# A transformer layer with two kinds of attention: adaLN's biases as initial values of its sums, the value weights' split in other places, the next key weights' load in another place

## The chip, the cores and the metric

The kernel runs on one core of a Trainium2 chip. Its time is device microseconds from start to end of one execution. Beside the plain runs there is one execution that the hardware profiler recorded; all rows below are from it.

A core has five engines, each with a queue of its own that it works through in order: TensorE (PE; its weight loads are shown apart as PEld), VectorE (DVE), ScalarE (ACT), GpSimd (POOL) and SyncE (SP), which here only issues transfers. An instruction that needs a result of another engine or of a transfer waits at the head of its queue, and all behind it waits too.

## The reference

One layer on a sequence of 1024 tokens with 1024 channels, in float32:

```
def hybrid_layer(x, c_act, w_ada, b_ada, w_in, rel_bias, g_a, g_b, w_out, w_up, conv_w, conv_b, w_down):
    mod = c_act @ w_ada + b_ada                      # c_act = silu(c)
    shift_mix, scale_mix, gate_mix, shift_ffn, scale_ffn, gate_ffn = jnp.split(mod, N_MOD, axis=-1)

    h = modulate(rms_norm(x), shift_mix, scale_mix)  # h * (1 + scale) + shift
    proj = h @ w_in                                  # (1024, 1024) @ (1024, 3072)
    qa, ka, va, qb, kb, vb = jnp.split(proj, cuts, axis=-1)
    oa = chunked_rel_attention(qa, ka, va, rel_bias) # 8 heads of 64
    ob = stick_breaking_attention(qb, kb, vb)        # 8 heads of 64
    mixed = jnp.concatenate([rms_norm(oa) * g_a, rms_norm(ob) * g_b], axis=-1) @ w_out
    x = x + gate_mix[:, None, :] * mixed

    h = modulate(rms_norm(x), shift_ffn, scale_ffn)
    gate, val = jnp.split(causal_depthwise_conv(h @ w_up, conv_w, conv_b), 2, axis=-1)
    return x + gate_ffn[:, None, :] * ((jax.nn.silu(gate) * val) @ w_down)

def reference(x, c, ...):
    x = hybrid_layer(x, jax.nn.silu(c), ...)         # DEPTH = 1
    return rms_norm(x) * final_g
```

The first line is the adaLN modulation: six vectors of 1024, each a product of the activated condition with a 1024x1024 part of `w_ada`, plus a bias. The change touches how the first two of them, shift and scale of the first sub-layer, get their biases, and how the first weights of `w_in` are made ready.

## The kernel before

Matrix products are made of three: each float32 operand is split into a high part in float32r and a low part, the rest; high x high, high x low and low x high are summed. A split is a copy on ScalarE (`wh`, for weights) and a subtraction on VectorE or GpSimd (`wl`).

The program has three parts. The first (lines 212 to 464, "phase 0") normalises x, transposes it, modulates it and makes q and k of the first pair of heads. The second is the attention with all other projections between its steps, the third the feed-forward part. The change lies in the first, with one function of the second.

Phase 0 goes over eight blocks `kb` of 128 channels. For each block `ada_sum(j, s)` on VectorE makes shift (s = 0) and scale (s = 1): the block's rows of `w_ada` lie as a 128x1024 tile `adaw`, and one multiply-reduce (lines 255 and 256, shown as CUSTOM_DVE, with a second instruction that reads the accumulator) sums them with the condition `cbc`. A small 128x1 instruction adds the bias (line 258), for scale also 1 (line 260). `trans0` on TensorE transposes the block of x into PSUM, half by half (`hf`, 512 tokens). `mod_hi` on ScalarE writes the modulated block twice, as high part `H` (line 302) and as float32 `mod` (line 303); `mod_lo` (line 308) subtracts them for the low part, on GpSimd, for block 7 on VectorE. `first_mm` on TensorE adds the block's products to four accumulators `a` (q and k, two halves): twelve products of 128x512 a block. Two buffers of `mod`, three of `t` and three of `adaw` bound how far the engines run apart.

The value weights of the first pairs come in two halves, loaded by `load_v0` (line 328) and split by `split_v0` (line 331), the first half's `wl` on VectorE, the second's on GpSimd, four pieces each. Loaded weights `raw` have two buffers, so that a load waits until the one before the last is split.

Then `evac_q0` and `evac_k0` copy the accumulators out. Each q half also goes by two transfers a head from one tile to another (lines 186 and 187), eight in all, each of which SyncE holds until its copy is there. The second part starts with `prefetch(0)` and `fill`: eight value tiles `mm` of 24 products each (`job_v`, line 498), with two PSUM buffers, whose results go out by two copies on ScalarE (line 512) and two subtractions on VectorE (line 513). `fill` also prefetches the next job's weights: the key weights of pair 1, by `pre_qk(1, 1)` (line 609), whose load and split stand where the scheduler puts them after the first value tile.

Nearly all of phase 0 is held in the order in which it is written (`ko`, `pe`); what is not held, as the `wl` pieces of `split_w`, the loads and the copies of q and k, is placed by a scheduler.

Of the kernel before, what the change touches and what calls it, by code (L numbers as in the profile page):

```python
# [11 lines left out]
F32 = mybir.dt.float32  # L12
F32R = mybir.dt.float32r
AF = mybir.ActivationFunctionType
ALU = mybir.AluOpType
# [4 lines left out]
P = 128  # L20
S = 1024
D = 1024
KB = D // P
# [32 lines left out]
def build(nc, tc, t, ctx):  # L56
    sy, ve, sc, gp, te = nc.sync, nc.vector, nc.scalar, nc.gpsimd, nc.tensor
    cnt = [0]

    def mk(pool, shape, dt, tag):  # L60
        cnt[0] += 1
        return pool.tile(shape, dt, name=f"{tag}_{cnt[0]}", tag=tag, bufs=BUFS.get(tag, 1))

    def pool(name, bufs=1, **k):
        c = tc.tile_pool(name=name, bufs=bufs, **k)
        return c, c.__enter__()
# [4 lines left out]
    f = lambda ap: ap.bitcast(F32)  # L71
# [10 lines left out]
    c0, p0 = pool("p0", side="left")  # L82
# [12 lines left out]
    bada = sm[:, 16:64]  # L95
# [17 lines left out]
    wst = p0  # L113

    def split_w(raw, shape, eng=gp):

        wh = mk(wst, shape, F32R, "wh")
        wl = mk(wst, shape, F32R, "wl")
        sc.copy(wh, raw)
        n = shape[1] // 4  # L120
        for i in range(0, shape[1], n):
            eng.tensor_sub(wl[:, i:i + n], raw[:, i:i + n], f(wh[:, i:i + n]))  # L122
        return wh, wl

    def load_w(src, shape):
        raw = mk(wst, shape, F32, "raw")
        r = sy.dma_start(raw, src)
        if hold[0]:
            tc.keep_in_program_order(r)
        return raw  # L130
# [5 lines left out]
    def pe(fn, *a, **k):  # L136
        r = fn(*a, **k)  # L137
        return tc.keep_in_program_order(r) if pin[0] else r
# [80 lines left out]
    gp.tensor_copy(smaskr, smask)  # L219
    sh_mix = mk(p0, [P, KB], F32, "sh_mix")  # L220
    sc_mix = mk(p0, [P, KB], F32, "sc_mix")

    def ada_load(j):
        w = mk(pst, [P, 2, D], F32, "adaw")
        for s in range(2):
            sy.dma_start(w[:, s], ada[j, :, s])
        return w

    ko = tc.keep_in_program_order
# [3 lines left out]
    cbc = mk(pst, [P, D], F32, "cbc")  # L233
# [17 lines left out]
    def ada_sum(j, s):  # L251

        w = aw[j][:, s]
        dst = (sh_mix, sc_mix)[s][:, j:j + 1]
        ko(ve.tensor_tensor_reduce(out=w, in0=w, in1=cbc, scale=1.0, scalar=0.0, op0=ALU.mult, op1=ALU.add,
                                   accum_out=dst))
        if s == 0:
            ko(ve.tensor_add(dst, dst, bada[:, j:j + 1]))
        else:
            ko(ve.scalar_tensor_tensor(dst, dst, 1.0, bada[:, 8 + j:9 + j], ALU.add, ALU.add))  # L260

    ssq0 = mk(p0, [P, TB], F32, "ssq0")
    m0 = mk(p0, [P, TB], F32, "ms0")
# [22 lines left out]
    def trans0(kb, hf, us=range(4)):  # L286
        if (kb, hf) not in tps:
            tps[kb, hf] = mk(ps0, [P, 4, P], F32, "t0")
        for u in us:
            pe(te.transpose, tps[kb, hf][:, u], xs[4 * hf + u][:, kb * P:(kb + 1) * P], ident)  # L290
# [7 lines left out]
    def mod_hi(kb, hf):  # L298
        tp = tps[kb, hf].rearrange("p a b -> p (a b)")
        dh, dl = hT[kb][hf]  # L300
        tmp = mk(pst, [P, HALF], F32, "mod0")
        ko(sc.activation(dh, tp, AF.Identity, scale=sc_mix[:, kb:kb + 1], bias=sh_mix[:, kb:kb + 1]))
        ko(sc.activation(tmp, tp, AF.Identity, scale=sc_mix[:, kb:kb + 1], bias=sh_mix[:, kb:kb + 1]))
        mods0[kb, hf] = tmp

    def mod_lo(kb, hf):
        dh, dl = hT[kb][hf]
        ko((ve if kb == KB - 1 else gp).tensor_sub(dl, mods0.pop((kb, hf)), f(dh)))

    def first_mm(kb, hfs):  # L310
        if kb == 0:
            for hf in hfs:
                for which in range(2):
                    acc0[which][hf] = mk(ps0, [P, HALF], F32, "a0")
        for n, (a, b) in enumerate(((0, 0), (0, 1), (1, 0)) if kb == 0 else ((0, 0), (1, 0), (0, 1))):
            for hf in hfs:
                for which in range(2):
                    pe(te.matmul, acc0[which][hf], w0[which][a][:, kb], hT[kb][hf][b],
                       start=kb == 0 and n == 0, stop=kb == KB - 1 and n == 2)

    def load_ada(j):
        aw[j] = ada_load(j)
# [4 lines left out]
    def load_v0(i):  # L327
        rv0.append(load_w(t["w_v"][0, i], [P, 4, 256]))

    def split_v0(i):  # L330
        wv0[0].append(split_w(rv0[i], [P, 4, 256], (ve, gp)[i]))


    acc0 = [[None, None], [None, None]]
    aw, raw0, rv0, wv0 = {}, [], [], [[]]
# [33 lines left out]
    norm_x(7)  # L369
    trans0(1, 0)  # L370
    ada_sum(0, 0)
    ada_sum(0, 1)
    scale_x(7)
    w0_hi(0)
# [8 lines left out]
    trans0(2, 0)  # L383
    w0_lo(1)
    ada_sum(1, 1)
    ada_sum(1, 0)
    ada_sum(2, 0)
# [26 lines left out]
    mod_lo(3, 0)  # L414
    ada_sum(5, 0)
    load_ada(7)
    trans0(4, 0)
    trans0(4, 1)
    trans0(5, 0)
# [21 lines left out]
    ada_sum(7, 0)  # L441
    trans0(7, 0)
    ada_sum(7, 1)
    mod_hi(7, 0)
    load_v0(1)
    first_mm(5, range(2))
    trans0(7, 1)
    mod_lo(7, 0)
    split_v0(0)
    mod_hi(7, 1)  # L450
    first_mm(6, range(2))
    mod_lo(7, 1)
    first_mm(7, [0])
    first_mm(7, [1])
    split_v0(1)
    sy.dma_start(rev_d, bass.AP(t["rev"].tensor, 0, [[ULEN, 8], [0, P], [1, ULEN]]))
    sy.dma_start(c_d, cbc[0:1])
    new_k(pairs[0])
# [148 lines left out]
        gate_out()  # L607

    def pre_qk(p, which):
        return [split_w(load_w(t["w_qk"][p, which], [P, KB, P]), [P, KB, P])]  # L610

    class Job:
# [9 lines left out]
    def add_k(p):  # L622
        add(lambda: pre_qk(p, 1), lambda w: job_qk(p, 1, (0, 1), w), 48 * 216, 16 * p - 18, 16 * p - 5)

    def add_q(p):

        got = []

        def pre():
            if not got:  # L630
                got.append(pre_qk(p, 0))
            return got[0]

        last = p == NP - 1
        add(pre, lambda w: job_qk(p, 0, (0,), w), 24 * 216, 16 * p - 10, 16 * p - 5)
        add(pre, lambda w: job_qk(p, 0, (1,), w), 24 * 216, 16 * p - (10 if last else 4), 16 * p - 3 if last else 16 * p + 3)
# [413 lines left out]
    for tb in range(4, TB):  # L1050
        for hf in range(2):
            n = 2 * (2 * (tb - 4) + hf - TR)
# [217 lines left out]
    def down_last(acts, ws):  # L1270

        done = None
        for tb in range(TB):
            c = slice(tb, tb + 1)
            o = mk(p2, [P, D], F32, "y")
            for hf in range(2):
                cc = slice(hf * HALF, (hf + 1) * HALF)
                xc = x2[tb][:, cc]
                n = (tb, hf) in by_half[:TL]
                down_mm(tb, hf, acts[n:], ws[n:])  # L1280
                junk = mk(p3, [P, HALF], F32, "Tc")
                ko(sc.activation(junk, xc, AF.Square, accum_out=ssqh[:, hf, c]))
                if hf == 0:
                    gp.tensor_mul(o[:, cc], xc, fg[0][:, cc])
                else:
                    ko(ve.tensor_scalar(m3[:, c], ssqh[:, 0, c], 1.0 / D, EPS, ALU.mult, ALU.add))
                    if done:
                        finish(*done)
                    ko(ve.scalar_tensor_tensor(m3[:, c], ssqh[:, 1, c], 1.0 / D, m3[:, c], ALU.mult, ALU.add))
                    gp.tensor_tensor(r3[:, c], m3[:, c], nhalf[:, c], ALU.pow)  # L1290
                yield
            done = tb, o
        finish(*done)
# [148 lines left out]
    w = []  # L1442
# [24 lines left out]
    for fb in range(2, NF):  # L1467
# [6 lines left out]
        if last:  # L1474
            dn = islice(dn, TL)
            out = chain(dn, down_last((act, act1), (wd, wd1)))
        act_fast(fb, w, dn, nw, nw1, ld, ld1, act1, out if last else dn, last)
        act, w, nw, wd, ld = act1, w1, nw1, wd1, ld1
# [39 lines left out]
```

## Time and profile before

| | |
|---|---|
| three runs | 1405.03, 1408.86, 1411.57 us; median 1408.86 |
| the profiled execution | 1405.52 us, span 1403.7 us, mean granted clock of TensorE 0.981 |
| busy, share of the span | PE 92%, DVE 82%, POOL 63%, ACT 44% |
| phase 0 | from 0 to 64 us of the span |
| its last products `a` | 63.33 us |
| first scores `S` of the attention | 83.88 us |

The shares are means over all parts. What the first 84 us spend is not seen in them; it is read from the order of time there. In a timeline row stand start, duration, engine, line, operation, tiles and, in brackets, how long the engine sat idle before it and what ended that.

### The profile page before, as it was taken

To read this page: it belongs to the slowest core of one execution; us is meant where nothing else is said; L and a number is where in the kernel's file an instruction comes from. 1 tells how busy PE (TensorE), PEld (TensorE's weight loads), DVE (VectorE), ACT (ScalarE), POOL (GpSimd) and SP (SyncE) were. 2 spreads that over 40 slices of the span, in tenths; PEclk is the share of its full clock that TensorE was granted. 3 is DMA by queue.
4 is the path that set the end of the run, shared out by engine and by line. 5 is a ranking of instruction groups with operands and counts; after the bars stand their busy time and mean duration, and the time that the engine had idled before them with its cause. 6 is when DMAs were issued, how large, how long until landed. Compare 5 with 4: busy or idle time off the path is not lost.

```text
span 1403.7 us, 19550 instructions
## 1 busy us (share of the span) xinstructions
PE 1296.4 (92%) x6596; PEld 1071.3 (76%) x6596; DVE 1155.9 (82%) x1943; ACT 624.3 (44%) x1286; POOL 880.5 (63%) x760
## 2 busy tenths in 40 slices
PE   4889998999899979998878999999999999999996
PEld 2678888898788967876656887777777777777774
DVE  6838897888677756857898899999989899989887
ACT  5646665666555544535433333333333333333334
POOL 4746676867533436654577777667677776676664
PEclk9999999999999998999999999999999999999998
DMA  8524635454463576663111111111211111112113
GB/s 306 183 92 121 166 84 156 125 148 135 119 173 100 166 203 191 219 230 126 38 31 38 53 46 45 60 53 46 65 49 45 46 45 60 53 46 67 46 38 120
DMA packets 73168, 145.07 MB, mean 103 GB/s; under 512 B 11114, under 2 KB 21482, under 8 KB 73068
## 3 DMA queue, kind: packets, MB, share of 16 engines
q1 hardware_dynamic: 73068, 143.83, 33.9%
q8 instruction: 52, 0.85, 0.3%
q14 instruction: 48, 0.39, 0.1%
HBM read 103.41 MB, written 18.88 MB: 87 GB/s over the span
## 4 chain that ended last, share of the span: by engine, by line
PE 33%; DVE 32%; ACT 7%; POOL 4%; issue 4%; DMA 3%; SPq 1%; POOLq 0%; ACTq 0%; DVEq 0%
PE up L1125 14%; DVE y L1134 9%; PE mm L137 8%; PE dnf L137 6%; PE T L137 4%; DVE x L1259 4%; ACT y L1130 3%; DVE y L1067 2%; DVE ah L1068 2%; PE S L137 2%; POOL pb L810 1%; DVE al L1069 1%; DMA rawm<-ada 1%; POOL wl L122 1%; ACT pb L786 1%
## 5 line engine op out<-in xcount | busy, mean ns | idle before, releaser
L1259 DVE TENSOR_TENSOR x<-dnf,x 128x512 f32<-128x512 f32 x340 | 222.6, 678 | 1.9 <-PE dnf L137 1.9
L1134 DVE SCALAR_TENSOR_TENSOR y<-y,sm,y 128x512 f32<-128x512 f32 (+2 forms) x160 | 189.3, 1183 | 26.1 <-ACT y L1130 26.1
L1091 POOL TENSOR_TENSOR wl<-raw,wh 128x1024 fp32r<-128x1024 f32 (+1 forms) x62 | 160.4, 2588 | 65.9 <-ACT wh L1089 65.9
L1125 PE MATMUL up<-h,wh 128*128 128x512 f32 x640 | 198.8, 392 | 1.2 <-DVE y L1195 0.8
L1130 ACT ACTIVATE y<-y,sm 128x512 f32<-128x512 f32 x80 | 65.3, 817 | 262.3 <-DVE y L1206 133.9
L137 PE MATMUL mm<-H,wh 128*128 128x512 f32 x448 | 149.5, 401 | 0.0
L137 PE MATMUL dnf<-dh,ah 128*128 128x512 f32 x336 | 133.8, 398 | 12.2 <-DVE x L1259 9.7
L810 POOL TENSOR_TENSOR pb<-pb,kt 128x512 f32<-128x512 f32 (+2 forms) x96 | 102.2, 1078 | 68.3 <-DVE kt L807 45.0
L1125 PEld LDWEIGHTS up<-h,wh 128*128 128x128 f32 x640 | 119.5, 189 | 29.1 <-ACT y L1167 2.2
L137 PE MATMUL dnf<-dl,ah 128*128 128x512 f32 x336 | 134.2, 399 | 2.5 <-POOL dl L1237 1.8
L137 PE MATMUL dnf<-dh,al 128*128 128x512 f32 x336 | 133.5, 397 | 0.9 <-DVE al L1069 0.9
L1125 PE MATMUL up<-h,wl 128*128 128x512 f32 x320 | 125.1, 391 | 0.0
L830 DVE TENSOR_TENSOR ptl<-T,pth 128x512 fp32r<-128x512 f32 (+2 forms) x192 | 98.4, 515 | 23.0 <-ACT pth L829 21.6
L803 POOL TENSOR_SCALAR pb<-pb,ri 128x640 f32<-128x640 f32 (+2 forms) x64 | 46.7, 730 | 104.2 <-DVE ri L802 60.9
L137 PE MATMUL mm<-wh,H 128*128 128x256 f32 x512 | 101.0, 289 | 7.1 <-DVE vs L513 7.1
L1237 POOL TENSOR_TENSOR dl<-modt,dh 128x512 fp32r<-128x512 f32 x42 | 64.8, 1544 | 67.4 <-ACT dh L1236 67.4
L829 ACT CAST pth<-T 128x512 fp32r<-128x512 f32 (+2 forms) x192 | 87.6, 459 | 41.4 <-PE T L137 39.9
L1125 PE MATMUL up<-Tc,wh 128*128 128x512 f32 x320 | 101.5, 399 | 4.3 <-ACT y L1151 4.3
L137 PE MATMUL T<-ident,pb 128*128 128x128 f32 x528 | 91.8, 278 | 14.3 <-POOL pb L810 5.9
L1234 POOL TENSOR_TENSOR modt<-modt,modt 128x512 f32<-128x512 f32 x44 | 69.6, 1582 | 54.6 <-DMA modt<-w_down 51.8
L807 DVE TENSOR_TENSOR_SCAN kt<-kt 128x128 f32<-128x128 f32 (+3 forms) x64 | 97.0, 1516 | 6.2 <-ACT kt L792 5.3
L137 PE MATMUL S<-kh,qs 128*128 128x384 f32 (+5 forms) x352 | 98.4, 361 | 3.9 <-ACT pb L786 3.9
(210 smaller groups left out, 3412.5 us busy)
## 6 DMA issues: line engine op xcount, KB each, us to landing
raw<-w_up SPq DMA_DIRECT2D x44, 512.0 KB, 3.5
rawm<-ada SPq DMA_DIRECT2D x64, 256.0 KB, 2.9
qs<-ex SPq DMA_DIRECT2D x104, 128.0 KB, 2.3
modt<-w_down SPq DMA_DIRECT2D x44, 256.0 KB, 3.2
adaw<-ada SPq DMA_DIRECT2D x16, 512.0 KB, 6.4
raw<-w_qk SPq DMA_DIRECT2D x16, 512.0 KB, 4.5
kh<-ex SPq DMA_DIRECT2D x56, 128.0 KB, 2.7
tbd<-wh SPq DMA_DIRECT2D x18, 256.0 KB, 2.3
```

What stands on the lines that cost most here:

```text
L137: r = fn(*a, **k)
L807: ve.tensor_tensor_scan(r, r, r, 1.0, ALU.mult, ALU.bypass)
L810: gp.tensor_mul(pt[:, a:b], pt[:, a:b], kt[:, a + 1:b + 1])
L829: sc.copy(dh, tp[:, 0:b - a])
L830: ve.tensor_sub(dl, tp[:, 0:b - a], f(dh))
L1091: late.append(lambda a=a, z=z: ko(gp.tensor_sub(wl[:, a:z], raw[:, a:z], f(wh[:, a:z]))))
L1125: ko(te.matmul(ps, w[x][:, kb], b[kb][y], start=start and n == 0, stop=n == 11, skip_group_check=True))
L1130: ko(sc.activation(y[:, a:z], src[:, a:z], AF.Identity, scale=cw[2][:, b], bias=cb[:, b]))
L1134: ko(ve.scalar_tensor_tensor(y[:, o:z], src[:, o - d:z - d], cw[2 - d][:, b], y[:, o:z], ALU.mult, ALU.add))
L1234: ko(gp.tensor_mul(raw, raw, gbc[hf]))
L1237: ko(gp.tensor_sub(wl, raw, f(wh)))
L1259: r = ve.tensor_add(xc, ps, xc)
```

## The change

Three edits. The bias goes into the sum: `ada_sum` gives it as the multiply-reduce's initial value, a per-partition operand, from `bada` for shift and from a new `bada1` (bias plus 1, one 128x8 instruction at the start) for scale; the sixteen 128x1 instructions are gone. The value weights' split is written out as `v0_hi` (cast) and `v0_lo` (one piece) and held in written order: the first half behind the last sum, the second behind the last products; `load_v0(1)` is written earlier. The key weights of pair 1 are loaded ahead of the stores of `rev` and `c` in the written order, and `pre_qk(1, 1)` uses that load.

```diff
--- before.py
+++ after.py
@@ -219,6 +219,8 @@
     gp.tensor_copy(smaskr, smask)
     sh_mix = mk(p0, [P, KB], F32, "sh_mix")
     sc_mix = mk(p0, [P, KB], F32, "sc_mix")
+    bada1 = mk(p0, [P, KB], F32, "bada1")
+    ve.tensor_scalar(bada1, bada[:, 8:16], 1.0, None, ALU.add)
 
     def ada_load(j):
         w = mk(pst, [P, 2, D], F32, "adaw")
@@ -251,13 +253,9 @@
     def ada_sum(j, s):
 
         w = aw[j][:, s]
-        dst = (sh_mix, sc_mix)[s][:, j:j + 1]
-        ko(ve.tensor_tensor_reduce(out=w, in0=w, in1=cbc, scale=1.0, scalar=0.0, op0=ALU.mult, op1=ALU.add,
-                                   accum_out=dst))
-        if s == 0:
-            ko(ve.tensor_add(dst, dst, bada[:, j:j + 1]))
-        else:
-            ko(ve.scalar_tensor_tensor(dst, dst, 1.0, bada[:, 8 + j:9 + j], ALU.add, ALU.add))
+        j = slice(j, j + 1)
+        ko(ve.tensor_tensor_reduce(out=w, in0=w, in1=cbc, scale=1.0, scalar=(bada, bada1)[s][:, j], op0=ALU.mult,
+                                   op1=ALU.add, accum_out=(sh_mix, sc_mix)[s][:, j]))
 
     ssq0 = mk(p0, [P, TB], F32, "ssq0")
     m0 = mk(p0, [P, TB], F32, "ms0")
@@ -327,8 +325,13 @@
     def load_v0(i):
         rv0.append(load_w(t["w_v"][0, i], [P, 4, 256]))
 
-    def split_v0(i):
-        wv0[0].append(split_w(rv0[i], [P, 4, 256], (ve, gp)[i]))
+    def v0_hi(i):
+        wv0[0].append((mk(wst, [P, 4, 256], F32R, "wh"), mk(wst, [P, 4, 256], F32R, "wl")))
+        ko(sc.copy(wv0[0][i][0], rv0[i]))
+
+    def v0_lo(i, n):
+        wh, wl = (x[:, n] for x in wv0[0][i])
+        ko((ve, gp)[i].tensor_sub(wl, rv0[i][:, n], f(wh)))
 
 
     acc0 = [[None, None], [None, None]]
@@ -414,6 +417,7 @@
     mod_lo(3, 0)
     ada_sum(5, 0)
     load_ada(7)
+    load_v0(1)
     trans0(4, 0)
     trans0(4, 1)
     trans0(5, 0)
@@ -441,18 +445,24 @@
     ada_sum(7, 0)
     trans0(7, 0)
     ada_sum(7, 1)
+    v0_hi(0)
     mod_hi(7, 0)
-    load_v0(1)
     first_mm(5, range(2))
     trans0(7, 1)
+    v0_lo(0, 0)
+    v0_lo(0, 1)
     mod_lo(7, 0)
-    split_v0(0)
+    v0_lo(0, 2)
+    v0_lo(0, 3)
     mod_hi(7, 1)
     first_mm(6, range(2))
     mod_lo(7, 1)
     first_mm(7, [0])
     first_mm(7, [1])
-    split_v0(1)
+    v0_hi(1)
+    for n in range(4):
+        v0_lo(1, n)
+    raw_k1 = [load_w(t["w_qk"][1, 1], [P, KB, P])]
     sy.dma_start(rev_d, bass.AP(t["rev"].tensor, 0, [[ULEN, 8], [0, P], [1, ULEN]]))
     sy.dma_start(c_d, cbc[0:1])
     new_k(pairs[0])
@@ -607,6 +617,8 @@
         gate_out()
 
     def pre_qk(p, which):
+        if (p, which) == (1, 1):
+            return [split_w(raw_k1[0], [P, KB, P])]
         return [split_w(load_w(t["w_qk"][p, which], [P, KB, P]), [P, KB, P])]
 
     class Job:
```

The order of instructions at two places. VectorE at the end of phase 0, from just behind the second sum of block 6 to the last subtraction of block 7 (`adaw` to `sh_mix` or `sc_mix` is a sum, the row behind it its accumulator's read; `wl` is a piece of the value weights' low part, H_112 and H_114 are the low parts of block 7), before:

```order
L122 TENSOR_TENSOR wl_494<-raw_334,wh_493 128x256
L260 SCALAR_TENSOR_TENSOR sc_mix_134<-sc_mix_134,sm_75 128x1
L255 ISA adaw_373,sh_mix_133<-adaw_373,cbc_143 128x1024
L255 ISA sh_mix_133 128x1
L122 TENSOR_TENSOR wl_494<-raw_334,wh_493 128x256
L258 TENSOR_TENSOR sh_mix_133<-sh_mix_133,sm_75 128x1
L255 ISA adaw_373,sc_mix_134<-adaw_373,cbc_143 128x1024
L255 ISA sc_mix_134 128x1
L260 SCALAR_TENSOR_TENSOR sc_mix_134<-sc_mix_134,sm_75 128x1
L308 TENSOR_TENSOR H_112<-mod_120_470,H_111 128x512
L308 TENSOR_TENSOR H_114<-mod_125_500,H_113 128x512
```

and now, from that sum on:

```order
L257 ISA adaw_340,sc_mix_134<-adaw_340,cbc_145,bada_49_135 128x1024
L257 ISA sc_mix_134 128x1
L257 ISA adaw_364,sh_mix_133<-adaw_364,cbc_145,sm_75 128x1024
L257 ISA sh_mix_133 128x1
L257 ISA adaw_364,sc_mix_134<-adaw_364,cbc_145,bada_49_135 128x1024
L257 ISA sc_mix_134 128x1
L334 TENSOR_TENSOR wl_459<-raw_327,wh_458 128x256 x2
L306 TENSOR_TENSOR H_112<-mod_124_461,H_111 128x512
L334 TENSOR_TENSOR wl_459<-raw_327,wh_458 128x256 x2
L306 TENSOR_TENSOR H_114<-mod_126_486,H_113 128x512
```

The four `wl` pieces have left the sums and stand around the two subtractions of block 7; the adds are gone, and the sums follow each other.

SyncE from the second value weights' load (`raw` from `w_v`) to the key weights' (the first `raw` from `w_qk`), before:

```order
L127 DMA raw_473<-w_v 128x1024
L456 DMA revd_61<-rev 1024x1x383
L457 DMA cd_62<-cbc_143 1x1024
L186 DMA qs_540<-qs_539 64x512
L187 DMA qs_540<-qs_539 64x512
L186 DMA qs_546<-qs_545 64x512
L187 DMA qs_546<-qs_545 64x512
L186 DMA qs_556<-qs_555 64x512
L187 DMA qs_556<-qs_555 64x512
L186 DMA qs_562<-qs_561 64x512
L187 DMA qs_562<-qs_561 64x512
L127 DMA raw_582<-w_qk 128x1024
```

and now:

```order
L127 DMA raw_367<-w_v 128x1024
L466 DMA revd_61<-rev 1024x1x383
L127 DMA raw_521<-w_qk 128x1024
L467 DMA cd_62<-cbc_145 1x1024
L186 DMA qs_528<-qs_527 64x512
L187 DMA qs_528<-qs_527 64x512
```

The key weights' load has moved ahead of the store of `c` and of the eight copies of q; it stays behind the store of `rev`. ScalarE in the same stretch, from the copies of q and k (`qs`, `kh`) to those of the first value tiles (`vs`), with the cast `wh` of the key weights, before:

```order
L184 ACTIVATE qs_545<-a_92_281 64x512
L184 ACTIVATE qs_555<-a_94_283 64x512
L184 ACTIVATE qs_561<-a_94_283 64x512
L512 CAST vs_591<-mm_593 128x2x64
L119 CAST wh_584<-raw_582 128x1024
L512 CAST vs_592<-mm_593 128x2x64
```

and now:

```order
L194 CAST kh_526<-a_96_281 64x512
L184 ACTIVATE qs_533<-a_93_278 64x512
L119 CAST wh_570<-raw_521 128x1024
L184 ACTIVATE qs_543<-a_95_280 64x512
L184 ACTIVATE qs_549<-a_95_280 64x512
L522 CAST vs_577<-mm_579 128x2x64
L522 CAST vs_578<-mm_579 128x2x64
```

The cast stood between the two copies of the first value tile, behind all copies of q; now it stands ahead of the last two copies of q.

## Rows read from the trace of the kernel before

**Rows 1.** Stages: us, busy (x count) by engine, TensorE's clock, DMA share, GB/s.

```profile
60.00:64.00 4.00, 3.69 (x15) 2.35 (x14) 2.07 (x4) 3.49 (x6) 2.71 (x4) 1.00 0.00 0
...
69.50:76.00 6.50, 0.21 (x2) 0.01 (x1) 0.63 (x3) 1.38 (x3) 0.52 (x1) 0.86 0.91 274
76.00:81.00 5.00, 4.96 (x23) 4.99 (x24) 0.38 (x2) 0.27 (x1) 2.28 (x4) 0.50 0.60 188
```

**Rows 2.** Groups on VectorE, 18 to 64 us: busy us, mean ns, idle before.

```profile
L255 DVE CUSTOM_DVE_ANT_0 adaw<-adaw,cbc 128x1024 f32<-128x1024 f32 x16 | 20.5, 1281 | 0.0
L260 DVE SCALAR_TENSOR_TENSOR sc_mix<-sc_mix,sm 128x1 f32<-128x1 f32 x8 | 6.1, 758 | 0.2
L258 DVE TENSOR_TENSOR sh_mix<-sh_mix,sm 128x1 f32<-128x1 f32 x8 | 5.2, 651 | 0.2
```

**Rows 3.** Timeline of TensorE, 51 to 84 us: start us, duration us.

```profile
51.55 3.05 PE L137 MATMUL a<-H,w 128*128 128x512 f32 x12
...
63.33 0.73 PE L137 MATMUL a<-H,w 128*128 128x512 f32 x2 [0.20 <-DVE H L308]
63.90 0.28 PE L137 MATMUL mm<-wh,H 128*128 128x256 f32 x1
...
69.43 0.28 PE L137 MATMUL mm<-wh,H 128*128 128x256 f32 x1
76.04 0.55 PE L137 MATMUL mm<-wh,H 128*128 128x256 f32 x1 [6.33 <-DVE vs L513]
...
83.88 0.33 PE L137 MATMUL S<-kh,qs 128*128 128x128 f32 x2
```

**Rows 4.** Timeline of ScalarE, 68 to 76 us.

```profile
68.09 0.59 ACT L184 ACTIVATE qs<-a 64x512 fp32r<-64x512 f32 x1 [0.97 <-DVE qs L185]
...
74.36 1.04 ACT L119 CAST wh<-raw 128x1024 fp32r<-128x1024 f32 x1 [5.38 <-DMA raw<-w_qk]
```

**Rows 5.** Timeline of SyncE's queue, 70 us.

```profile
70.44 1.07 SPq L127 DMA_DIRECT2D raw<-w_qk  x2
```

**Rows 6.** Timeline of VectorE, 29 to 58 us.

```profile
29.04 1.22 DVE L255 CUSTOM_DVE_ANT_0 adaw<-adaw,cbc 128x1024 f32<-128x1024 f32 x1
30.19 0.08 DVE L255 DVE_READ_ACCUMULATOR2_ANT sh_mix<- 128x1 f32 x1
...
30.38 1.22 DVE L255 CUSTOM_DVE_ANT_0 adaw<-adaw,cbc 128x1024 f32<-128x1024 f32 x1
...
34.02 1.21 DVE L255 CUSTOM_DVE_ANT_0 adaw<-adaw,cbc 128x1024 f32<-128x1024 f32 x1
...
47.79 1.21 DVE L255 CUSTOM_DVE_ANT_0 adaw<-adaw,cbc 128x1024 f32<-128x1024 f32 x1
...
51.85 2.31 DVE L255 CUSTOM_DVE_ANT_0 adaw<-adaw,cbc 128x1024 f32<-128x1024 f32 x1
54.09 0.08 DVE L255 DVE_READ_ACCUMULATOR2_ANT sc_mix<- 128x1 f32 x1
...
57.30 1.12 DVE L260 SCALAR_TENSOR_TENSOR sc_mix<-sc_mix,sm 128x1 f32<-128x1 f32 x1
```

**Rows 7.** Timeline of GpSimd, 32 to 53 us.

```profile
32.02 21.05 POOL L308 TENSOR_TENSOR H<-mod,H 128x512 fp32r<-128x512 f32 x10 [5.31 <-ACT mod L303]
```

**Rows 8.** Single lines: duration in ns, least/median/most, first and last start, forms.

```profile
L863 DVE SCALAR_TENSOR_TENSOR otl<-o,sm,oth x32: 474/792/1359, 106.5 to 621.9; 128x256 fp32r<-128x256 f32 x32
...
L122 DVE TENSOR_TENSOR wl<-raw,wh x4: 412/414/1487, 48.9 to 55.6; 128x256 fp32r<-128x256 f32 x4
...
L122 POOL TENSOR_TENSOR wl<-raw,wh x92: 715/738/2189, 61.3 to 649.2; 128x256 fp32r<-128x256 f32 x92
...
L1134 DVE SCALAR_TENSOR_TENSOR y<-y,sm,y x160: 740/1182/1843, 765.4 to 1376.7; 128x512 f32<-128x512 f32 x80, 128x511 f32<-128x511 f32 x40, 128x510 f32<-128x510 f32 x40
```

**Rows 9.** Loads issued at 70.4 and at 43.0 us: size, us to landing.

```profile
raw<-w_qk SPq DMA_DIRECT2D x1, 512.0 KB, 3.9
...
raw<-w_v SPq DMA_DIRECT2D x1, 512.0 KB, 9.1
```

## The prediction before the run

> **What bounds the kernel now.** I read the table of stages first, then the groups and the order of time on the engines that it points to. The part ahead of the attention is one chain, and two places in it are long. The one shows in the stages: from 69.5 to 76 us TensorE works 0.21 of 6.50 us, and from 76 to 81 us it works 4.96 of 5.00 but at a granted clock of 0.50, its 1.2 GHz level; from 60 to 64 us it had 1.00 (2.4 GHz) [rows 1]. The other shows in the groups: VectorE's sixteen adaLN sums, each a 128x1024 multiply-reduce, have no idle time in front of them [rows 2], and ScalarE, GpSimd and TensorE wait for what they give, down to the last product `a` (lines 310 to 318) at 63.33 us.
>
> TensorE's pause is 6.33 us long and was ended by VectorE's `vs` of the first value tile [rows 3]. Behind that stands ScalarE: its queue has the copy of the next key weights between the two copies of that tile, and it sat 5.38 us for the load of those weights [rows 4]. SyncE issued that load only at 70.44 us, behind q's eight copies [rows 5]. So what is late last is not the copying of `vs` but one 512 KB load.
>
> **The adds.** The first part of the change takes away sixteen 128x1 adds, 6.1 + 5.2 = 11.3 us of busy time [rows 2]. That is not what it gives back. In the open, with GpSimd idle, sums start 1.34 us apart (29.04 to 30.38); without the add the next can start where the accumulator's read starts, 30.19, so 0.19 is saved [rows 6]. Five sums stand in the open (both of block 0, both of block 1, the first of block 2): 0.9 us. From 32.02 us GpSimd works without a gap through ten subtractions of 128x512 [rows 7], and an add takes about 1.1 us. There the two engines take turns: six sums from 34.02 to 47.79 are 2.295 us apart. The sum at 51.85 has no add before it, only a weight subtraction, and it took 2.31 us itself, with its read at 54.09, 2.24 after its start [rows 6]. So without the add the sum waits in its place: 2.295 becomes 2.24, and seven such sums (second of block 2 to block 5) save 0.4 us.
>
> The Trainium skill (SBUF — State Buffer, "Who interferes with whom") says that a VectorE instruction with two SBUF inputs and a GpSimd instruction that reads SBUF shut each other out for the whole instruction. By that rule the 1.1 us belong to GpSimd and stay; read as VectorE's own work they would all go, which is the first rival below. The 2.31 us of the sum at 51.85 bears the rule out.
>
> The sums now start from a per-partition operand. The trace has no such sum. The nearest rows are a 128x256 operation with two SBUF inputs and a per-partition operand, 0.474 us at least, and the same size without it, 0.412 [rows 8]: 0 to 0.06 each, 0 to 1.0 us for sixteen. A gain is excluded, since the stream of elements is the same. I take 0, and keep the other end for the range. The one new 128x8 instruction at the start costs nothing: VectorE waits there for the load of `c`.
>
> **The value weights.** Before, four subtractions `wl` stand among the last four sums; each gives GpSimd another turn. From the start of the sum at 47.79 to the end of the last add (57.30 + 1.12 = 58.42) pass 10.63 us [rows 6]. Now four sums follow each other: three steps of 2.24, then 1.15 to the last read and 0.08 for it, 7.95 us. Saved: 2.7. They are paid in part behind the sums. Before, the last add and the last product (63.33 + 0.73 = 64.06 [rows 3]) are 5.64 apart. Now GpSimd's two subtractions of block 6 come with one `wl` between: a turn of GpSimd is 2.24 - 1.15 = 1.09, `wl` 0.41 [rows 8], so 2.6 us, and then TensorE has fourteen products left at 3.05 / 12 = 0.254 us [rows 3], 3.55. That is 6.15, 0.5 more than before. ScalarE's cast of 1.04 us, now ahead of block 7's pair, and the other three `wl` run beside these products. The second value weights' cast goes behind block 7's last pair, to about 59.2, and GpSimd's four `wl`, 0.74 each [rows 8], end from 59.9 to 62.2; TensorE starts the value tiles at 60.4 and wants them from twelve products of 0.118 later, 61.8 to 62.9: nothing, or the cast's 1.04 if it comes that late. The earlier line for their load leaves SyncE's order as it was. If VectorE's cover is gone and each of its four `wl` meets a turn of GpSimd, it costs 4 x 1.09 = 4.4 us. The sum: 0.9 + 0.4 + 2.7 - 0.5 = 3.5 us, bounds -0.9 and the rival's; the last product ends at 60.56.
>
> **The key weights.** Their load now stands in SyncE's queue ahead of the store of `c` and of q's eight copies. It needs the buffer of the first value weights, so it waits for VectorE's last `wl`: 54.42 (58.42 less 4.0) + 2.6, one `wl`, block 7's subtraction (0.8, estimated as twice a `wl`) and two `wl`, about 59.0. What is queued behind it on SyncE is not ready before 60. Between 60 and 64 us the DMA engines moved nothing [rows 1], so I take 3.9 us to landing, as the same load had, against 9.1 for the value weights in a crowded stretch [rows 9]: 62.9. On ScalarE the cast now stands after four copies of k and two of q. Before, the place after the second q copy came at 68.09 - 0.97 - 0.59 = 66.53 [rows 4], 2.47 behind the last product: now 63.0. The load is in by then, narrowly. Behind the cast (1.04) come two q copies (0.59, a wait of up to 0.97 for VectorE, 0.59) and two `vs` copies with their subtractions; one such took 76.04 - 75.40 = 0.64 [rows 3, 4]. So TensorE goes on 3.4 us after the cast, at 67.5. Its first two value tiles end 69.71 - 64.06 = 5.65 behind the last product, 66.2 now. The pause shrinks from 6.33 to about 1.25 us: 5.1 saved. The next 48 products took 7.84 us (76.04 to 83.88); at full clock 48 take 5.65 (47 steps from 63.90 to 69.43 are 5.53) [rows 3]. With no long pause I expect no fall of the clock: 2.2 saved.
>
> **The sum.** 3.5 + 5.1 + 2.2 = 10.8 us. Behind this TensorE is back to back (4.96 of 5.00 us already from 76 on [rows 1]), and all five queues keep their order but for one background load, so the rest of the program moves as a whole and nothing gives the time back. The profiled execution took 1405.52 us (span 1403.7), so 1394.7; the three runs' median is 1408.86, 3.3 above it, and by that the time is 1398.0. What is late next is VectorE's sums, as before.
>
> **Rivals.**
> *The adds were VectorE's own time.* Then all 11.3 us go in place of 1.3: 20.8 saved, 1388. For it: they show as busy. Against: the sum at 51.85 and the even 2.295.
> *The first stage gains nothing.* The `wl` meet GpSimd's turns at the end, where lines 440 to 455 are tight, and eat the 3.5. Then the pause and the clock remain, 7.3: 1401.6. For it: VectorE and GpSimd take turns wherever both have work.
> *The load is no earlier where it matters.* If SyncE gets the buffer late, or the transfer takes the 9.1 us, it lands at 68.1, 5.1 late; two q copies and two `vs` now stand behind the cast, so TensorE pauses over 6 us again and the clock falls as before. Only the 3.5 remain: 1405.4. Against: the empty DMA.
> *Slower: the per-partition operand puts the sum into a slower form.* The place is all sixteen sums, which are on the path. The slowest nearby kind, a 128x512 operation with such an operand, has a median of 1.182 us [rows 8]; twice that for 1024 elements is 2.36, 1.15 over the 1.21 of a sum: 18.4 us, 7.6 in sum lost, 1416.5. It decides from 10.8 / 16 = 0.68 us each. Against: that median includes waits for GpSimd, its minimum is 0.740.
>
> **How the numbers follow.** Forecast 0.57, no gain in the first stage 0.19, late load 0.12, adds gone wholly 0.07, slower form 0.05. 0.5% is 7.0 us, about what a measurement of this kernel tells from no change. Faster by more: 0.50 of the forecast's 0.57, 0.10 of the second's 0.19, the adds' 0.07, 0.02 of the late load: 0.69. Slower: 0.05. The rest, 0.26, is the same. The range is 1390 to 1406: down to 1390 for a first stage that gives 8 us more, up to the late load; the forecast's own range is 1394 to 1402.
>
> **What would show it.** Right: sums about 1.15 apart in the open and 2.24 beside GpSimd; the last product `a` near 60.6 us; ScalarE idle under 1 us before its key-weight cast; TensorE's pause at the third value tile under 2 us, the clock at 1.00 behind it, and the first `S` near 73 us. Wrong: sums beside GpSimd near 1.2 us (first rival), a last product at 64 (second), several idle us before the cast (third), sums over 1.5 us in the open (fourth), or a first `S` at 73 with the gain lost later in the attention.

## The result: 1408.8 to 1398.0 us, and the profile after

| | before | after |
|---|---|---|
| runs, median | 1408.83 us (1404.34 to 1411.57, 7 runs) | 1398.0 us (1397.06 to 1401.45, 7 runs) |
| ratio | | 0.9934, 95% interval 0.9916 to 0.9952 |
| the profiled execution | 1405.52 us, span 1403.7, clock 0.981 | 1397.97 us, span 1396.2, clock 0.978 |
| first `S` of the attention | 83.88 us [rows 3] | 73.45 us |

The forecast was 1398.0. Repeated in two later series, each beside the kernel before on one chip, the ratio was 0.9926 (0.9902 to 0.9951) and 0.9929 (0.9911 to 0.9948): 10.6 and 10.2 us in the medians, after 10.8 here.

The stages first, as in [rows 1]: time, then busy time by engine, TensorE's clock, the DMA share, GB/s.

```profile
60.00:64.00 4.00, 4.00 (x35) 3.91 (x34) 3.52 (x6) 3.24 (x6) 1.86 (x3) 1.00 0.52 182
69.50:76.00 6.50, 6.50 (x60) 6.50 (x59) 1.50 (x5) 1.41 (x6) 0.51 (x2) 1.00 0.77 255
76.00:81.00 5.00, 5.00 (x45) 5.00 (x45) 2.22 (x6) 2.26 (x9) 1.25 (x4) 1.00 0.00 0
```

From 69.5 to 76 us TensorE is busy throughout where it had worked 0.21 of 6.50, and from 76 to 81 us the clock is 1.00 where it had been 0.50. There is traffic from 60 to 64 now, where there was none: the key weights' load, issued at 58.64 us, landed 3.7 us later. What the DMA engines move from 69.5 to 76 us (255 GB/s) are now other loads.

TensorE's timeline, answering to [rows 3]:

```profile
57.07 3.53 PE L137 MATMUL a<-H,w 128*128 128x512 f32 x14 [0.18 <-POOL H L306]
60.44 0.28 PE L137 MATMUL mm<-wh,H 128*128 128x256 f32 x1
...
67.91 0.36 PE L137 MATMUL mm<-wh,H 128*128 128x256 f32 x1 [1.86 <-DVE vs L523]
...
73.45 0.34 PE L137 MATMUL S<-kh,qs 128*128 128x128 f32 x2
```

The last product `a` ends at 60.60, the pause is 1.86 us in place of 6.33, and the 48 products behind it take 5.54 us in place of 7.84. SyncE's queue, to [rows 5], and ScalarE's, to [rows 4]:

```profile
58.64 0.33 SPq L127 DMA_DIRECT2D raw<-w_qk  x1
```

```profile
62.45 0.59 ACT L184 ACTIVATE qs<-a 64x512 fp32r<-64x512 f32 x1
63.07 1.05 ACT L119 CAST wh<-raw 128x1024 fp32r<-128x1024 f32 x1
...
65.50 0.59 ACT L184 ACTIVATE qs<-a 64x512 fp32r<-64x512 f32 x1 [0.75 <-DVE qs L185]
66.11 0.27 ACT L522 CAST vs<-mm 128x128 fp32r<-128x128 f32 x1
67.17 0.43 ACT L522 CAST vs<-mm 128x128 fp32r<-128x128 f32 x2 [0.79 <-DVE vs L523]
```

The load goes out 11.8 us earlier, and the cast has no wait in front of it. A new small wait stands at 67.17: the second `vs` copy waits for VectorE's first `vs` subtraction.

VectorE's sums are shown as groups (to [rows 2]; the 16 adds are gone) and in the timeline (to [rows 6]), and GpSimd's subtractions beside them (to [rows 7]):

```profile
L257 DVE CUSTOM_DVE_ANT_0 adaw<-adaw,cbc,bada 128x1024 f32<-128x1024 f32 x8 | 15.2, 1914 | 0.0
L257 DVE CUSTOM_DVE_ANT_0 adaw<-adaw,cbc,sm 128x1024 f32<-128x1024 f32 x8 | 15.1, 1910 | 0.0
```

```profile
29.69 1.28 DVE L257 CUSTOM_DVE_ANT_0 adaw<-adaw,cbc,sm 128x1024 f32<-128x1024 f32 x1
...
30.90 1.28 DVE L257 CUSTOM_DVE_ANT_0 adaw<-adaw,cbc,bada 128x1024 f32<-128x1024 f32 x1
32.10 0.08 DVE L257 DVE_READ_ACCUMULATOR2_ANT sc_mix<- 128x1 f32 x1
32.10 2.29 DVE L257 CUSTOM_DVE_ANT_0 adaw<-adaw,cbc,sm 128x1024 f32<-128x1024 f32 x1
...
45.46 2.30 DVE L257 CUSTOM_DVE_ANT_0 adaw<-adaw,cbc,sm 128x1024 f32<-128x1024 f32 x1
...
52.14 2.29 DVE L257 CUSTOM_DVE_ANT_0 adaw<-adaw,cbc,bada 128x1024 f32<-128x1024 f32 x1
54.36 0.08 DVE L257 DVE_READ_ACCUMULATOR2_ANT sc_mix<- 128x1 f32 x1
```

```profile
31.33 25.69 POOL L306 TENSOR_TENSOR H<-mod,H 128x512 fp32r<-128x512 f32 x12 [5.05 <-ACT mod L301]
```

The sums' busy time rose from 20.5 to 30.3 us, yet they end earlier: each now carries in its own duration the wait for GpSimd that the adds had carried. In the open they start 1.21 apart (29.69 to 30.90) and last 1.28 where they had lasted 1.22. Beside GpSimd they are 2.23 apart (six steps from 32.10 to 45.46).

### The profile page after: what moved, and what is told of

It is laid out like the page before. It is cut to its first block, busy times and chain, and to the rows that moved or that the text cites. A ratio compares the mean times of both kernels' runs of the same rounds, so it can differ in the third digit from the quotient of the medians.

```text
span 1396.2 us, 19540 instructions
## 1 busy us (share of the span) xinstructions
PE 1303.4 (93%) x6596; PEld 1076.2 (77%) x6596; DVE 1152.9 (83%) x1928; ACT 625.5 (45%) x1286; POOL 881.5 (63%) x760
## 4 chain that ended last, share of the span: by engine, by line
PE 42%; DVE 34%; ACT 8%; POOL 7%; issue 5%; DMA 4%; SPq 0%; POOLq 0%; DVEq 0%; ACTq 0%
PE up L1137 13%; PE mm L137 13%; DVE y L1146 9%; PE dnf L137 6%; PE T L137 6%; DVE x L1271 4%; ACT y L1142 3%; PE S L137 3%; DVE y L1079 2%; DVE ah L1080 2%; POOL H L306 2%; POOL pb L822 2%; POOL wl L122 1%; DVE kt L819 1%; DVE al L1081 1%
## 5 line engine op out<-in xcount | busy, mean ns | idle before, releaser
L1137 PE MATMUL up<-h,wh 128*128 128x512 f32 x640 | 201.9, 397 | 1.1 <-DVE y L1207 0.8
```

What stands on the lines that cost most here:

```text
L1137: ko(te.matmul(ps, w[x][:, kb], b[kb][y], start=start and n == 0, stop=n == 11, skip_group_check=True))
```

## The experiments

My theory: an add's 1.1 us was a turn of GpSimd, which the sum now waits out itself, so the adds and the value split give some 1.5 and 2 us, in the first stage only; the key load gives the rest, and the lead at the first `S` stays to the end. Rivals: the adds were VectorE's own time; one part does all; the lead is given back later, as the profiled pair hints (7.55 us where the medians have 10.8).

The first three each do one part alone.

**The adds alone.**

```
- ... scalar=0.0, ..., accum_out=dst))         + the two adds of lines 258 and 260
+ ... scalar=(bada, bada1)[s][:, j], ..., accum_out=(sh_mix, sc_mix)[s][:, j]))
```

> The adds alone: the sixteen biases as initial values, the value weights' split and the key weights' load as before. Theory (beside GpSimd an add's 1.1 us was GpSimd's turn, which the next sum now waits out): five sums in the open start about 1.2 us apart in place of 1.34, those beside GpSimd 2.23 in place of 2.295; the last product a ends about 1 us earlier, near 63; TensorE's pause of 6.3 us and the low clock behind it stay; about 1 us less in all. Rival (the 11.3 us of adds were VectorE's own work): sums 1.2 us apart everywhere, last product near 54, about 10 us less.

Measured: 1403.90 us (10 runs) against 1405.16, ratio 0.9992 (0.9970 to 1.0014). TensorE's timeline:

```profile
61.86 0.73 PE L137 MATMUL a<-H,w 128*128 128x512 f32 x2 [0.19 <-DVE H L306]
...
74.70 0.55 PE L137 MATMUL mm<-wh,H 128*128 128x256 f32 x1 [6.66 <-DVE vs L511]
...
81.78 0.34 PE L137 MATMUL S<-kh,qs 128*128 128x128 f32 x2
```

The last product ends 1.5 us earlier, and the pause stays. On VectorE six sums beside GpSimd, from 32.07 to 45.42 us, start 2.23 apart, and those in the open 1.20: the rival, with 1.2 everywhere, does not hold. Taking 11.3 us of busy time away gives 1.5 on the path, and the runs can't tell that from nothing.

**The value split alone** (`split_v0` taken apart, its pieces and `load_v0(1)` put where the changed kernel has them; adds and key load as before).

```
-    split_v0(0)
+    v0_hi(0)      # ahead of block 7's first pair; its four v0_lo(0, n) behind the last sum, among mod_lo(7, hf)
-    split_v0(1)
+    v0_hi(1)      # behind block 7's last pair, then v0_lo(1, 0..3)
```

> The value weights' split alone, adds and key load as before. Theory: the last four sums follow each other without the pieces between, last product 2.2 us earlier, near 61.9; the pause of 6.3 us and the low clock stay since the key load is still behind q's copies; first S near 81.7, about 2 us less in all. Rival (the pieces meet GpSimd's turns at the end instead): last product at 64, nothing gained.

Measured: 1403.96 us (10 runs), ratio 0.9994 (0.9977 to 1.0010).

```profile
58.53 3.53 PE L137 MATMUL a<-H,w 128*128 128x512 f32 x14 [0.30 <-POOL H L308]
...
74.22 0.55 PE L137 MATMUL mm<-wh,H 128*128 128x256 f32 x1 [6.71 <-DVE vs L524]
...
82.49 0.34 PE L137 MATMUL S<-kh,qs 128*128 128x128 f32 x2
```

The last product ends at 62.06, 2.0 us earlier; the pause stays. 1.5 and 2.0 add up to the 3.46 of both. The first `S` is only 1.4 earlier: in this execution the 48 products behind the pause took 8.27 us where they had taken 7.84, at a clock that stayed near 0.50 for longer.

**The key load alone.**

```
+    raw_k1 = [load_w(t["w_qk"][1, 1], [P, KB, P])]      # ahead of the store of c and of q's copies
...
+        if (p, which) == (1, 1):
+            return [split_w(raw_k1[0], [P, KB, P])]
```

> The key weights' load alone, adds and value weights as before. Theory: last product unchanged at 64.06; load issued soon after VectorE's last piece of the value weights, near 56 us, and there before ScalarE's cast at 66.5; TensorE's pause 1.9 us in place of 6.33, clock 1.00 behind it, first S near 77.3 in place of 83.88, about 6.6 us less in all. Rival (the clock falls whatever the pause, or the pause is set by something else): first S at 79.5 or later, 4.4 us less or nothing.

Measured: 1400.80 us (10 runs), ratio 0.9969 (0.9947 to 0.9991): the one part that the runs show by itself. The profiled execution, at 1406.36 us, is the slowest of the ten. TensorE's timeline and its stages:

```profile
71.16 0.36 PE L137 MATMUL mm<-wh,H 128*128 128x256 f32 x1 [1.86 <-DVE vs L514]
...
78.35 0.33 PE L137 MATMUL S<-kh,qs 128*128 128x128 f32 x2
```

```profile
69.50:76.00 6.50, 4.84 (x28) 4.87 (x29) 1.69 (x6) 1.10 (x5) 0.83 (x4) 0.74 0.89 214
76.00:81.00 5.00, 5.00 (x46) 5.00 (x46) 1.44 (x5) 1.15 (x5) 0.51 (x2) 1.00 0.46 179
```

The pause shrank to the same 1.86 us as in the changed kernel, yet here the clock fell (0.74 from 69.5 to 76), and the first `S` was 1.05 later than expected. That is a miss: a pause of 1.86 us is no safe bound. The load went out at 55.90 us and the cast stood at 66.32, as expected.

In the medians the three parts alone gave 1.3, 1.2 and 4.4 us, 6.9 together, where all at once gave 10.2 to 10.8. With intervals of some 3 us or more on each part, the runs can't say whether the parts add up.

**GpSimd's reads taken away**, in the kernel before. Blocks 0 to 6 lose their low parts, which are left out: GpSimd fills them with zeros and reads nothing.

```
-        ko((ve if kb == KB - 1 else gp).tensor_sub(dl, mods0.pop((kb, hf)), f(dh)))
+        if kb == KB - 1:
+            ko(ve.tensor_sub(dl, mods0.pop((kb, hf)), f(dh)))
+        else:
+            mods0.pop((kb, hf))
+            ko(gp.memset(f(dl), 0.0))
```

> The kernel before, with GpSimd's fourteen subtractions (blocks 0 to 6) replaced by memsets of the same tiles, which read nothing; the low parts of those blocks are left out. Theory (an add's 1.1 us beside GpSimd is the wait for a GpSimd instruction that reads): all sixteen adds take about 0.16 us and the sums start 1.34 us apart everywhere, so the last sum ends near 48 us in place of 57.3 if the loads of adaLN's weights keep up. Rival (the adds are slow by themselves from 33 us on, as for the loads or the write beside ScalarE's reads): they stay at 1.1 us and 2.295 apart.

Measured: one run, 1394.99 us, against 1406.16. GpSimd's and VectorE's timelines:

```profile
20.42 8.21 POOL L312 MEMSET H<- 128x512 f32 x14
```

```profile
21.44 0.16 DVE L260 SCALAR_TENSOR_TENSOR sc_mix<-sc_mix,sm 128x1 f32<-128x1 f32 x1
...
27.87 0.16 DVE L260 SCALAR_TENSOR_TENSOR sc_mix<-sc_mix,sm 128x1 f32<-128x1 f32 x1
...
33.30 1.22 DVE L255 CUSTOM_DVE_ANT_0 adaw<-adaw,cbc 128x1024 f32<-128x1024 f32 x1
...
34.55 0.16 DVE L260 SCALAR_TENSOR_TENSOR sc_mix<-sc_mix,sm 128x1 f32<-128x1 f32 x1
...
41.41 1.23 DVE L255 CUSTOM_DVE_ANT_0 adaw<-adaw,cbc 128x1024 f32<-128x1024 f32 x1 [1.12 <-DMA adaw<-ada]
```

GpSimd is done at 28.63, and every add takes 0.15 to 0.16 us, where beside GpSimd's subtractions it had taken 1.1. So that 1.1 us was GpSimd's turn. It takes a GpSimd that reads: the adds at 21.44 and 27.87 ran beside its memsets and took 0.16 us too. The last sum ends at 48.98, near the 48 expected; sums now wait for their loads (1.12 us at 41.41).

**The key weights' cast behind the first two value tiles' copies**, in the changed kernel; otherwise that kernel.

```
-            sc.copy(vh, src)
+            r = sc.copy(vh, src)
+            if g == 0 and tb < 2:
+                ko(r)
...
+        if g == 0 and tb == 1:
+            kw1[0] = split_w(raw_k1[0], [P, KB, P], gp, True)      # the cast held here
...
```

> The changed kernel, with the cast of the key weights held on ScalarE behind the copies of the first two value tiles, where before it stood ahead of the last two copies of q. Theory (ScalarE's order of copies sets the rest of the pause): the pause of 1.86 us shrinks by the cast's 1.05 to about 0.8, first S near 72.4, about 1 us less than the changed kernel. Rival (VectorE's subtractions of q set it): pause unchanged.

Measured: 1396.79 us (6 runs), ratio 0.9957 (0.9938 to 0.9975).

```profile
66.69 0.36 PE L139 MATMUL mm<-wh,H 128*128 128x256 f32 x1 [1.00 <-DVE vs L528]
...
72.23 0.34 PE L139 MATMUL S<-kh,qs 128*128 128x128 f32 x2
```

The pause is 1.00 us, 0.2 more than expected, and the first `S` 1.2 earlier than in the changed kernel. The medians do not show it: 8.4 us below the kernel before, where the changed kernel had 10.8 in a series of its own. That q's two copies and the `vs` pairs make up what is left of the pause is not tested.

**The changed kernel again**, without an edit, for the question whether its lead sinks at the same places.

> The changed kernel once more. Theory (the first 84 us repeat, what differs later is where the clock falls): last product near 60.6, pause 1.86, first S near 73.4 within 0.3; clock falls after 200 us at other places, and over all runs the time goes up with the lost clock. Rival (the change itself costs 3 us later in the attention): the lead over the kernel before sinks at the same places, 230 to 300 us, in this execution too, whatever the clock does there.

Measured: 1395.59 us (6 runs) against 1406.16, ratio 0.9926 (0.9902 to 0.9951), first `S` at 73.22. Against the first profile of before its lead was 10.7 us at the first `S` and 7.8 near 301, much as in the first pair. Two executions that agree look like a property of the kernel; the later runs show that they are not.

**The condition read from PSUM by the sums**, on top of the late cast; the transposes have two buffers in place of three to make room.

```
-    ... "t0": 3, ...
+    ... "t0": 2, ...
-        ko(ve.tensor_tensor_reduce(out=w, in0=w, in1=cbc, ...
+        ko(ve.tensor_tensor_reduce(out=w, in0=w, in1=cps_[0], ...      # a 128x1024 tile in PSUM
...      # and the copies to cbc are gone
```

> The changed kernel with the later cast, and the broadcast condition read by the sums from PSUM, where TensorE's product left it, in place of a copy in SBUF (two PSUM buffers for the transposes in place of three to make room). Theory (a sum with one SBUF input takes no turns with GpSimd): sums about 1.25 us apart everywhere, last sum before 46 us; then TensorE's own work is the bound, last product near 55 in place of 60.3, first S near 67.5, about 5 us less than with the later cast alone. Rival (PSUM input or the two transpose buffers cost as much): last product at 60 or later.

Measured: 1393.90 us (6 runs), ratio 0.9922 (0.9901 to 0.9943). VectorE, GpSimd and TensorE, and the changed kernel's first products `a` for comparison:

```profile
30.90 1.27 DVE L260 CUSTOM_DVE_ANT_0 adaw<-adaw,cb,sm 128x1024 f32<-128x1024 f32 x1
...
32.10 1.27 DVE L260 CUSTOM_DVE_ANT_0 adaw<-adaw,cb,bada 128x1024 f32<-128x1024 f32 x1
...
33.90 1.28 DVE L260 CUSTOM_DVE_ANT_0 adaw<-adaw,cb,bada 128x1024 f32<-128x1024 f32 x1 [0.52 <-DMA adaw<-ada]
```

```profile
30.13 3.96 POOL L309 TENSOR_TENSOR H<-mod,H 128x512 fp32r<-128x512 f32 x3 [2.83 <-ACT mod L304]
```

```profile
30.11 1.12 PE L139 MATMUL t<-ident,xs 128*128 128x128 f32 x4 [3.57 <-ACT mod L304]
30.87 4.88 PE L139 MATMUL a<-H,w 128*128 128x512 f32 x12
...
44.63 0.66 PE L139 MATMUL t<-ident,xs 128*128 128x128 f32 x4 [1.10 <-ACT mod L304]
...
55.59 5.82 PE L139 MATMUL a<-H,w 128*128 128x512 f32 x24
```

```profile
24.76 3.91 PE L137 MATMUL a<-H,w 128*128 128x512 f32 x12
```

With one operand in PSUM the turns are gone on both sides: sums 1.20 apart while GpSimd works, GpSimd's subtractions 1.32 each (3.96 / 3) where they had been 2.14 (25.69 / 12). The last sum's read is at 46.04, 8.3 us earlier. But the last product ends at 61.4, later than in the changed kernel, where I had expected 55: another miss. The transposes, which have lost a buffer, now wait for ScalarE to read the tiles before them, 9.7 us in four waits where the changed kernel has 3.3 in three. The products `a` stand behind them in TensorE's queue and begin at 30.87 us in place of 24.76. From there to the end TensorE has one gap, of 1.10 us. So VectorE is no longer the bound, but TensorE starts 6.1 us late and has no slack to make that up, and nothing was gained. The sums from PSUM with three transpose buffers were not tried.

**Four more on one chip, before at 1404.90 (7 runs):** the kernel before profiled again, the late cast, the changed kernel, and the PSUM form, each without a new edit.

> The kernel before, unchanged, profiled a second time. Its first S starts near 83.9 us by every theory. Theory 'the falls of the clock belong to places of the program': TensorE's granted clock falls to 0.50 near 238, 262 and 347 us here (the changed kernel's places at 228, 252 and 337, each 10.5 later), which the first profile of this kernel did not show at the first two places, and the value of the changed kernel's lead at 300 us is 9 to 11 us against this profile. Rival 'the kernel before does not fall there, the changed kernel gives 3 us of its lead back because it comes earlier': no fall between 80 and 340 us, as in the first profile, and a lead of 7.5 us at 295.

> The changed kernel with the key weights' cast held behind the copies of the first two value tiles, beside the changed kernel and the kernel before on one chip. If the 1 us by which its first S comes earlier (72.2 against 73.4) is kept to the end: 0.6 to 1.4 us below the changed kernel in the same call. Rival 'covered by the clock's scatter': within 1.5 us of it on either side.

> The changed kernel, unchanged, as the measure for the others of this call. 10 to 11 us below the kernel before, ratio 0.992 to 0.994; first S near 73.3, TensorE's pause at the third value tile 1.85 us.

> The changed kernel with the late cast and the condition read from PSUM by the sums, two transpose buffers instead of three. Its first S is 0.2 us later than the changed kernel's, so by the first stage alone it is 0 to 0.5 us slower than it in the same call; the rival, that its lower median of the earlier call (1393.90 against 1395.59) is its own, has it 1 to 2.5 us faster again.

Measured: before 1405.67 in its one run, its first `S` at 82.91, 1.0 earlier than in its first profile; late cast 1393.47 (4 runs), ratio 0.9918 (0.9898 to 0.9938); changed 1394.74 (4 runs), 0.9929 (0.9911 to 0.9948); PSUM form 1394.96 (4 runs), 0.9921 (0.9905 to 0.9938). So neither variant can be told from the changed kernel: the late cast is 1.3 us lower with an overlap of the intervals (its first `S` is at 72.58, the changed kernel's at 73.19), and the PSUM form, 1.7 lower in the first series, is 0.2 higher in this one.

Where the lead goes shows in two stretches of the attention, in the stages' columns, here before and before again, changed and changed for the third time:

```profile
220.00:270.00 50.00, 44.98 (x277) 39.28 (x276) 40.56 (x62) 31.58 (x74) 36.46 (x46) 1.00 0.47 124
330.00:400.00 70.00, 62.83 (x397) 56.07 (x396) 52.61 (x162) 37.81 (x97) 37.81 (x47) 0.95 0.53 138
```

```profile
220.00:270.00 50.00, 44.96 (x263) 38.94 (x263) 40.54 (x62) 31.47 (x73) 36.39 (x46) 0.97 0.46 125
330.00:400.00 70.00, 63.48 (x413) 56.46 (x412) 53.68 (x166) 39.35 (x102) 38.82 (x47) 0.98 0.56 144
```

```profile
220.00:270.00 50.00, 45.41 (x254) 38.99 (x253) 39.77 (x52) 30.15 (x67) 38.40 (x46) 0.93 0.49 132
330.00:400.00 70.00, 62.74 (x385) 56.06 (x384) 50.09 (x170) 35.07 (x96) 32.23 (x43) 0.93 0.52 132
```

```profile
220.00:270.00 50.00, 45.40 (x263) 39.08 (x262) 40.97 (x55) 31.62 (x70) 40.45 (x50) 0.97 0.53 144
330.00:400.00 70.00, 63.06 (x394) 55.22 (x392) 52.14 (x181) 37.34 (x104) 34.13 (x49) 0.98 0.55 149
```

From 220 to 270 us the granted clock differs between executions of one kernel about as much as between the kernels: 1.00 and 0.97 for before, 0.93 and 0.97 for the changed one, whose second execution had 0.93 as well. A single line of the attention, with its first and last start, shows how far executions drift apart; changed, and changed for the third time (before has 106.5 to 621.9 in [rows 8]):

```profile
L875 DVE SCALAR_TENSOR_TENSOR otl<-o,sm,oth x32: 475/766/1076, 96.0 to 613.0; 128x256 fp32r<-128x256 f32 x32
```

```profile
L875 DVE SCALAR_TENSOR_TENSOR otl<-o,sm,oth x32: 475/766/1077, 95.8 to 605.9; 128x256 fp32r<-128x256 f32 x32
```

Two executions of the same kernel, 0.2 us apart at 96, are 7.1 apart at 613. Against the first profile of before the one has lost 1.6 us of its 10.5 by then, the other has gained 5.3 on its 10.7. Of the two theories for the second profile of before, neither holds as it was put: the clock fell at one of the two early places (0.57 from 260 to 264 us, but 1.00 from 236 to 240), not at both and not at none.

Whether it is the clock can be estimated from all five executions. Summed in stretches of 2 us, the clock that was not granted from 106 to 622 us is 10.2 and 13.6 us in the two of before, and from 96 to 612 us it is 13.7, 11.9 and 6.8 us in the three of the changed kernel. From the first to the last start of this line pass 515.4 and 517.1 us in before, and 517.0, 516.7 and 510.1 in the changed kernel. What is left without the lost clock is 503.3 to 505.2 us in all five. So by this estimate the change costs nothing that shows later in the attention, and the lead of the first pair sinks because its second execution lost more clock (13.7 against 10.2).

## Why the prediction was right

**The two waits and the arithmetic.** At the first `S` the lead was 83.88 - 73.45 = 10.43 us, with 10.8 forecast, and the medians of three series moved by 10.8, 10.6 and 10.2. So what is gained ahead of the attention stays in the medians. The profiled pair alone showed a sign of being wrong that the prediction names, a gain lost later in the attention (10.43 at the first `S`, 7.55 at the end); it goes with the clock that each execution lost.

That 1398.0 was met to the tenth is luck. Seven runs of one kernel spread over 4 to 7 us, and the kernel before has its first `S` at 82.91 in its second profile, which makes the lead 9.5. The step from the profiled execution to the median held because the median of before stayed at 1408.83 in this series; in the later ones it was 1404.90 to 1406.16, and the changed kernel came to 1394.74 and 1395.59.

**The first stage** gave 64.06 - 60.60 = 3.46, with 3.5 forecast, but two of its terms were off and cancelled. To the end of the sums the changed kernel gained 58.42 - 54.44 = 3.98 (forecast 4.0), as follows. VectorE began its sums 0.16 earlier. The five open steps gave 0.65 (0.13 each), not 0.9: the per-partition operand, which I took at 0, cost the upper bound, 0.06 a sum. The sixth sum gave 1.11, which the forecast did not have: it started at 30.90, before GpSimd, and kept its 1.20, while its add in the kernel before met GpSimd for a full turn. The six contended steps gave 0.41 (forecast 0.4). The last four sums gave 1.65, not 2.7: the forecast let the very last one run alone in 1.15, but it met GpSimd too (2.29 at 52.14), which now had work to the end. In the kernel before, GpSimd had been idle from 53.07 to 56.13, and the last two sums had run in 1.21 each. Behind the sums the forecast had 6.15 us to the last product; it was 6.16.

By the Trainium skill (SBUF — State Buffer, "Who interferes with whom") a VectorE instruction with two SBUF inputs and a GpSimd instruction that reads SBUF exclude each other, and a VectorE instruction with at most one SBUF input, outside the two-port modes, does not contend. The runs agree with both halves: 1.1 against 0.16 us for an add with and without GpSimd's reads, 2.23 against 1.20 between sums with the condition in SBUF and in PSUM. So the first rival (all 11.3 us go) fell: the sixteen sums grew from 20.5 to 30.3 us as the adds went.

**The key weights.** Issue 58.64 (forecast 59.0), cast at 63.07 without a wait (63.0). The pause was 1.86, not 1.25. The mis-sized term is the 3.4 us from the cast's end to the third value tile; it was 67.91 - 64.12 = 3.79, because the second `vs` copy waited 0.79 for a subtraction that stood behind q's on VectorE. I had carried over a pair's 0.64 us from a place where VectorE was free. The rest of the 0.6 is that the first two value tiles took 5.46 us behind the last product and not 5.65, and that the cast began 0.07 later. Apart from the earlier last product, the step gave 4.67 us where 5.1 were forecast.

**The clock.** No fall, 48 products in 5.54 us: 2.30 gained, 2.2 forecast. This was the less certain term, more so than the text had it, and it came out in part by luck: with the same pause of 1.86 us the clock fell in the execution with the key load alone, and did not fall in three of the changed kernel.

**The other rivals.** The first stage did not come to nothing (3.46). The load was not late (3.7 us to landing, 3.9 forecast). The slower form of the sum did not come: 0.06 us each, a tenth of the 0.68 at which it would decide. The 7.0 us that the prediction took for the least a measurement can tell was too much: ten runs told the 4.4 us of the key load alone from nothing.

## What to carry to other kernels

A tiny instruction that takes seven times its usual duration may be waiting for its turn beside another engine, and then removing it hands that wait to its neighbour: price it at its duration in the open, 0.16 us here, and not at 1.1. A load that everything waits for is found by asking what released the pause, then what stood ahead of its issue in its queue; by itself, moving one load of 512 KB brought the first `S` 5.5 us forward, and taking away 11 us of busy time 2.1. When two profiles differ by a few us far from the change, compare each kernel with a second execution of itself before looking for a cause.

## What was not expected of the hardware

- A per-partition initial value costs a 128x1024 multiply-reduce 0.06 us in the open (1.22 to 1.28). With the second operand in PSUM as well it took 1.27; a sum from PSUM without such a value was not run.
- With one operand in PSUM the sums and GpSimd's subtractions ran beside each other at full speed: 1.20 and 1.32 us, from 2.23 and 2.14.
- A sum that was already running when GpSimd began, at 31.33 us, kept its duration (30.90, 1.28), and only the next one took turns.
- Beside a GpSimd that only writes (memsets until 28.63 us), the adds kept their 0.16 us.
- Two executions of one kernel differ by up to 7 us at 613 us, as much as the clock that they lost on the way differs (13.7 and 6.8 us, an estimate; 0.93 against 0.97 from 220 to 270 us, 0.93 against 0.98 from 330 to 400). What sets off such a fall, the runs leave open.
